# Layer 2 keys and values turned by VectorE in blocks and through DRAM, states in column groups of TensorE, and a planner in which VectorE and GpSimd exclude each other

## The chip, the cores and the metric

The kernel runs on one core of a Trainium2 chip. A core has five engines with queues of their own: TensorE (PE; its weight loads are shown as PEld), VectorE (DVE), ScalarE (ACT), GpSimd (POOL) and SyncE (SP), which here only issues DMAs. TensorE multiplies a stationary block (the weights, here up to 128 rows by 128 columns) with moving columns and writes to PSUM, which the kernel uses as eight banks of 128 x 512 float32. The metric is the device time of one execution in microseconds (us), as a median of several runs. A time of the profile is counted from the start of the span, the stretch that the profiler records.

## The reference

Two layers work on 1024 prompt tokens and on 8 sequences of 4 sample tokens with a state of their own, together 1056 tokens (TOK) of 1024 features. What is computed, cut to what matters:

```
xn = rmsnorm(x);  u = xn @ a_w_in                          # first layer: RG-LRU
xb, gate = u[:, :1536], u[:, 1536:]
xc = causal convolution of xb, 4 taps
r, i = sigmoid(block-diagonal products of xc + bias)
a = exp(-8 * softplus(-lam) * r)
h[t] = a[t] * h[t-1] + sqrt(1 - a[t]**2) * i[t] * xc[t]
x = x + (h * silu(gate)) @ a_w_out

xn = rmsnorm(x);  q, f, v, gate = split(xn @ b_w_in, 4)    # second layer: HGRN2, 8 heads of 128
g = lb + (1 - lb) * sigmoid(f);  k = 1 - g;  q = silu(q)   # a gate for each of the 128 key features
S[t] = diag(g[t]) @ S[t-1] + outer(k[t], v[t])             # a 128 x 128 state per head
o[t] = q[t] @ S[t]
x = x + (rmsnorm(o) * silu(gate)) @ b_w_out
y = rmsnorm(x)
```

The outputs are y and the final states of both layers, for the prompt and for the samples.

## The kernel before, in words

**Layout.** Activations lie with the features on the 128 partitions and the tokens along the free dimension. A product is made as three matmuls of rounded parts (`mm3`, lines L243 to L245: high by high, high by low, low by high), and each operand is split into a high and a low part on the other engines (`subtract`, L325). The first layer works in three chunks of 352 tokens, in the second most products go in quarters of 264 tokens.

**The planner.** The program of each layer isn't issued in the order of the source. Every operation is put into a `Flow` with its engine, an estimated time, the keys that it reads and writes and a priority. `Flow.plan` is a list scheduler: it takes again and again the engine that is free first and of its ready operations the one with the smallest key. `Flow.back` plans from the end backward, the resulting times become the keys of the next forward plan, and the best of nine forward plans sets the order in which every engine's instructions are emitted. `HOP` is the delay that the planner puts between engines, `side` an extra for TensorE work that isn't of the main chain. Main products (`main=True`) keep the order of the source. An operation marked `both` is one of VectorE that the planner stretches if GpSimd is busy. `search` changes keys at random, and keeps what lets an early operation of TensorE end no later; before the change only the first layer's flow uses it. A plan is only an order: on the chip every instruction waits for what it really depends on.

**Start.** 48 matmuls of ones (L729) stand ahead of the first products of layer 1; their result is not used.

**Layer 2.** The first two heads use plain products of 352 columns. For heads 2 to 7 `seven` forms two of the four projections at once, in seven products of half size in place of eight: the sums of the activations are built once (`add`, L1368, and a split), the sums of the weights for each head (`combine`, L1438). The sums of the seven products are made by VectorE as it reads them from PSUM (`plus`, L1501), over a ring of three banks. Each head has four bursts of other TensorE work between these products:

- burst 1: the parts of the attention matrix between neighbouring tokens (`levels01`: L1052 with L1072), and for the head before `keys_` and `values`;
- burst 2: the same over distances of 2 and 4 (`levels24`: L1052, L1086), `states` for the head before (L1217, and for the samples L1225), and `advance` (L1246);
- burst 3: `outs` for the head before (L1271, L1273), `advance`, and `levels816` (L1052, L1106);
- burst 4: `gated` for the head before, `levels3264`, and half of `values`.

Within a head the gates of tokens are multiplied up in a tree (`scale`: query and key rows in L1034, the gates themselves in L1043), level by level, and each burst needs the levels made after the burst before. `own_gate` (L1064) is the first step: queries times gates. `scale(h, 64, ...)` after burst 4 leaves in row B2 the keys, scaled to the end of their chunk of 128 tokens.

**Turning.** `states` computes for each chunk of 128 tokens the product of its keys and values, summed over tokens, so both are needed with tokens on the partitions. `transposed` has TensorE turn 128 x 128 blocks against an identity matrix into a PSUM bank (L1161, four to a bank), and ScalarE copies the bank to SBUF (L1167). That is done for all keys in burst 1 (8 blocks) and for the values in burst 4 (4 blocks) and burst 1 (4 blocks). `samples` does the same for the sample tokens (L1173). `states` then runs eight matmuls of 128 x 128 (L1217), and VectorE adds chunk after chunk with its decay (into `SA`). `kt` shares its buffer with `on`, the normed outputs that burst 4 turns back.

**DMA.** Nearly all transfers go through SP's queue, in the order of the plan (the helper `dma`, L312): the weights of `seven` into the slots `wraw` and a part of `R`, the states of the samples in (`si`) and out (`out_ss`), the gated outputs to a scratch in DRAM (`yd`).

The functions concerned, with their line numbers:

## Time and profile before

| | |
|---|---|
| three runs | 1072.68, 1069.47, 1072.20 us, median 1072.2 |
| profiled execution | 1069.42 us, its span 1067.3 us |
| granted clock of TensorE, mean | 0.996 |
| TensorE busy | 1054.5 us, 99% of the span |
| TensorE weight loads | 1026.1 us, 96% |
| VectorE busy | 816.2 us, 76% |
| ScalarE busy | 589.2 us, 55% |
| GpSimd busy | 526.4 us, 49% |
| instructions of TensorE | 9964 matmuls, as many weight loads |
| moved by DMA | 103.06 MB, mean 97 GB/s |

How to read it: busy time counts instructions that run, not those that wait. The page divides the span into 40 slices of 26.7 us and gives the busy share of each engine in each slice as a digit. The chain of waits follows the work that ended last back to the start, from each instruction to what released it. The timeline lists groups of neighbouring instructions of a kind: start and duration in us, engine, line, operation, the tiles written and read, and in square brackets how long the engine stood idle ahead of it and what ended that. In the tables by windows each engine has its busy microseconds, with the number of instructions in brackets, then the granted clock, the share of the DMA engines and the GB/s.

### The profile page before, as it was taken

The page shows a single profiled execution, that of the slowest core. Times are in us where ns is not written, and L with a number is a line of the kernel's source. Part 1 is how long each engine was busy: PE and PEld are TensorE (multiplying, and loading weights), DVE is VectorE, ACT ScalarE, POOL GpSimd, SP SyncE. Part 2 cuts the span into 40 slices and gives each one's busy share as a digit, 9 for nine tenths or more (in the row PEclk, how much of TensorE's full clock was granted, in tenths as well). Part 3 has the DMA queues.
Part 4 walks back from the last instruction along what each step waited for, and adds up shares of the span by engine and source line. Part 5 has one row for each costly group of instructions (what it writes and reads, how often), then busy time and mean ns, then how long its engine had stood idle before and what let it go on. Part 6 is the DMA issues. An engine that isn't in the chain of part 4 may idle for free.

```text
span 1067.3 us, 25614 instructions
## 1 busy us (share of the span) xinstructions
PE 1054.5 (99%) x9964; PEld 1026.1 (96%) x9964; DVE 816.2 (76%) x1610; ACT 589.2 (55%) x1340; POOL 526.4 (49%) x601
## 2 busy tenths in 40 slices
PE   9999999999999999999989999999999999999997
PEld 9999999999999999999989999999999999999986
DVE  7999995788888689264798987877868686883436
ACT  6569656877675875243344464646464554652324
POOL 3426443444634365555657555555545455552544
PEclk9999999999999999999999999999999999999998
DMA  9201112123752585440211121212121212374204
GB/s 294 67 20 52 57 47 74 56 60 97 228 173 61 171 282 179 126 131 28 80 33 40 44 91 46 90 44 91 44 92 51 74 62 65 123 214 127 78 8 163
DMA packets 70120, 103.06 MB, mean 97 GB/s; under 512 B 9200, under 2 KB 50160, under 8 KB 70000
## 3 DMA queue, kind: packets, MB, share of 16 engines
q1 hardware_dynamic: 67696, 98.67, 29.6%
q10 hardware_dynamic: 2304, 2.77, 0.7%
q8 instruction: 78, 1.28, 0.5%
q14 instruction: 42, 0.34, 0.1%
HBM read 71.05 MB, written 25.49 MB: 90 GB/s over the span
## 4 chain that ended last, share of the span: by engine, by line
PE 90%; DVE 6%; issue 1%; DMA 1%; POOL 1%; ACT 0%; ACTq 0%; POOLq 0%; DVEq 0%
PE mm L243 25%; PE mm L244 24%; PE mm L245 24%; PE hg L1052 1%; PE hg L569 1%; PE hg L1271 1%; DVE R L1368 1%; PE hg L1217 1%; PE hg L1161 1%; PE hg L243 1%; PE hg L245 1%; PE hg L244 1%; PE hg L1273 1%; DMA wraw<-in_w_dram 1%; PE mm L1052 1%
## 5 line engine op out<-in xcount | busy, mean ns | idle before, releaser
L243 PE MATMUL mm<-xh,whi 128*128 128x352 f32 (+1 forms) x1143 | 359.5, 315 | 0.0
L244 PE MATMUL mm<-xl,whi 128*128 128x352 f32 (+1 forms) x1143 | 354.8, 310 | 0.0
L245 PE MATMUL mm<-xh,wlo 128*128 128x352 f32 (+1 forms) x1143 | 354.7, 310 | 0.0
L325 POOL TENSOR_TENSOR wlo<-wraw,whi 128x256 fp32r<-128x256 f32 (+3 forms) x184 | 199.2, 1100 | 189.7 <-ACT whi L380 104.5
L244 PEld LDWEIGHTS mm<-xl,whi 128*128 128x128 f32 x1143 | 215.8, 189 | 1.7
L243 PEld LDWEIGHTS mm<-xh,whi 128*128 128x128 f32 x1143 | 215.5, 189 | 1.8
L245 PEld LDWEIGHTS mm<-xh,wlo 128*128 128x128 f32 x1143 | 215.5, 189 | 0.0
L501 DVE SCALAR_TENSOR_TENSOR k<-xb,prm_sb,k 128x352 f32<-128x352 f32 (+2 forms) x144 | 89.2, 629 | 14.8 <-ACT k L498 10.8
L243 PE MATMUL mm<-t,whi 128*128 128x264 f32 (+1 forms) x306 | 89.4, 292 | 0.5 <-DVE k L1501 0.5
L244 PE MATMUL mm<-t,whi 128*128 128x264 f32 (+1 forms) x306 | 87.7, 287 | 0.0
L245 PE MATMUL mm<-t,wlo 128*128 128x264 f32 (+1 forms) x306 | 87.6, 286 | 0.0
L1501 DVE TENSOR_TENSOR k<-mm,k 128x264 f32<-128x264 f32 x144 | 60.4, 428 | 34.5 <-PE mm L245 32.7
L584 POOL TENSOR_TENSOR k<-X 128x352 f32<-128x352 f32 x36 | 44.4, 1243 | 45.1 <-DVE R L585 34.3
L325 POOL TENSOR_TENSOR wlo<-R,whi 128x256 fp32r<-128x256 f32 x64 | 51.8, 830 | 25.4 <-ACT whi L1428 25.4
L380 ACT CAST whi<-wraw 128x512 fp32r<-128x512 f32 (+2 forms) x83 | 45.9, 574 | 26.4 <-PE mm L244 18.7
L243 PEld LDWEIGHTS mm<-t,whi 128*128 128x128 f32 x306 | 57.6, 188 | 1.2 <-DVE k L1501 0.9
L245 PEld LDWEIGHTS mm<-t,wlo 128*128 128x128 f32 x306 | 57.6, 188 | 0.0
L244 PEld LDWEIGHTS mm<-t,whi 128*128 128x128 f32 x306 | 57.6, 188 | 0.0
L243 PE MATMUL mm<-yh,whi 128*128 128x352 f32 x153 | 49.9, 326 | 0.0
L1428 ACT CAST whi<-wraw 128x512 fp32r<-128x512 f32 x52 | 32.0, 616 | 31.7 <-PE mm L245 17.4
L244 PE MATMUL mm<-yl,whi 128*128 128x352 f32 x153 | 49.4, 323 | 0.0
L245 PE MATMUL mm<-yh,wlo 128*128 128x352 f32 x153 | 49.4, 323 | 0.0
(478 smaller groups left out, 2601.3 us busy)
## 6 DMA issues: line engine op xcount, KB each, us to landing
wraw<-in_w_dram SPq DMA_DIRECT2D x90, 256.0 KB, 2.7
wraw<-in_wo_dram SPq DMA_DIRECT2D x34, 192.0 KB, 2.5
si<-in_s_in_dram SPq DMA_DIRECT2D x8, 512.0 KB, 3.6
out_ss_out_dram<-si SPq DMA_DIRECT2D x8, 512.0 KB, 2.8
R<-in_w_dram SPq DMA_DIRECT2D x15, 256.0 KB, 2.5
sg<-x1b SPq DMA_DIRECT2D x21, 176.0 KB, 2.8
x<-sg SPq DMA_DIRECT2D x21, 176.0 KB, 1.8
R<-td SPq DMA_DIRECT2D x72, 44.0 KB, 1.9
```

The source lines that it names most:

```text
L243: T.matmul(out, wh, xh, start=first, stop=False)
L244: T.matmul(out, wh, xl, start=False, stop=False)
L245: T.matmul(out, wl, xh, start=False, stop=last)
L325: emit = lambda: e.tensor_tensor(b, x, a.bitcast(F32), op=ALU.subtract)
L380: act(m, lambda hi=hi, raw=raw, m=m: S.copy(hi[:, :m], raw[:, :m]), rk, (hk,), prio)
L501: dve(u, lambda src=src, dst=dst, sh=sh, k=k: V.scalar_tensor_tensor(dst, sh(src, k), pc("cw", 12 * k + m), dst, op0=ALU.mult, op1=ALU.add ...
L569: fl.add("PE", 0.62, lambda ps=ps, i=i, c=c: T.matmul(ps[:96, :CH], gs[:, i, :], ST[:96, chunk(c)], start=True, stop=True), (("gs",), *((" ...
L584: pool(CH, lambda x=x, a=a, b=b: G.tensor_tensor(x, a.bitcast(F32), b.bitcast(F32), op=ALU.add), (ak, bk), (xk,), 3)
L1052: T.matmul(ps[32 * j:32 * j + 32, n * w:n * w + w], B[:, o:o + 32], q(slice(o, o + 32)), start=True, stop=True, tile_position=(0, 32 * j))
L1161: T.transpose(ps[:, n * 128:(n + 1) * 128], row[:, a:a + 128], ident)
L1428: act(512, lambda: S.copy(hi, raw), (rk,), (hk,), 2)
L1501: dve(QT, lambda: V.tensor_tensor(o[0], z[0], u[0], op=ALU.add), (z[1], u[1]), (o[1],), 0)
```

## The change

It has two parts.

**The planner.** `HOP` becomes a number for each engine. A Flow can be given `busy`, the times at which the engines are free as it begins; layer 2's is made from the log of layer 1's. In `plan` an operation of VectorE marked `both` starts to run only when the last operation of GpSimd is through (less 0.085 us), and an operation of GpSimd only when the last marked one of VectorE is through (less 0.05 us). The estimated times of many operations are other numbers. An empty operation of GpSimd writes the keys of the gate row ahead of layer 2, and layer 2's flow is searched too. The order of the main products, what the operations compute and how many there are is the same for layer 1.

**Layer 2.** `transposed` is gone. `turned` has VectorE turn a row of 1024 tokens by 32 x 32 blocks (one instruction of 128 x 1024, L1166 in the new file), writes the 512 KB to a scratch in DRAM, of which there are two for keys and two for values, and reads them back with four DMAs of 128 KB, one for each group of 32 partitions, so that whole columns of tokens lie on the partitions. It is called behind burst 4 for values and keys. In `kt` and `vt` the 128 features of a chunk are then four runs of 32. `states` takes the keys as four weight blocks of 32 columns, each in a column group of its own (`tile_position=(0, 32 * a)`), so there are 32 matmuls of 128 x 32 weights a bank in place of 4 of 128 x 128 (32 in place of 8 a head; the trace counts two instructions for each of these float32 matmuls). The values are read as four runs of 32 columns, in `states` and in `outs`.

```diff
-    HOP = 0.2
+    HOP = {"PE": 0.22, "DVE": 0.14, "ACT": 0.14, "POOL": 0.14, "SP": 0.2}
...
-    def __init__(self, until=None, side=1.2):
+    def __init__(self, until=None, side=1.2, busy=None):
...
+        self.busy = {e: (busy or {}).get(e, 0.0) for e in self.ENGINES}
...
-        return self.HOP + b[6] + (2.15 + a[5] / 250.0 if a[5] else 0.0)
+        return self.HOP[a[0]] + b[6] + (2.15 + a[5] / 250.0 if a[5] else 0.0)
...
-        free = dict.fromkeys(self.ENGINES, 0.0)
-        dma = 0.0
+        free = dict(self.busy)
+        dma = locked = taken = 0.0
...
-            if both and free["POOL"] > t0:
-                us = max(us, free["POOL"] - t0 + us - 0.13)
+            if both:
+                us += max(0.0, taken - t0 - 0.085)
+                locked = t0 + us
+            elif e == "POOL":
+                us += max(0.0, locked - t0 - 0.05)
+                taken = t0 + us
...
-            fl.add("ACT", 0.25 + 0.0007 * n + more, emit, r, w, prio)
+            fl.add("ACT", 0.08 + 0.00086 * n + more, emit, r, w, prio)
...
-            fl.add("DVE", 0.13 + 0.0011 * n, emit, r, w, prio, both=both)
+            own = 0.13 if "scalar_tensor_tensor" in emit.__code__.co_names else 0.075
+            fl.add("DVE", own + 0.00104 * n, emit, r, w, prio, both=both)
...
-            fl.add("POOL", 0.1 + 0.00245 * n, emit, r, w, prio)
+            fl.add("POOL", 0.13 + 0.0022 * n, emit, r, w, prio)
...
-        fl = Flow(side=0.4)
+        last = {e: max(t[3] for t in fl.log if t[1] == e) for e in Flow.ENGINES}
+        fl = Flow(side=0.4, busy={e: max(0.0, t - last["PE"]) for e, t in last.items()})
...
+        fl.add("POOL", 0.0, lambda: None, (), GK, 0)
...
-        def transposed(row, rk, dst, key, parts):
-
-            got = []
-            for i in parts:
-                ps, pk = next(hg)
-
-                def emit(i=i, ps=ps):
-                    for n in range(4):
-                        a = (4 * i + n) * 128
-                        T.transpose(ps[:, n * 128:(n + 1) * 128], row[:, a:a + 128], ident)
-
-                pe(0.49, emit, rk, (pk,))
-                got.append((i, ps, pk))
-            yield
-            for i, ps, pk in got:
-                act(512, lambda i=i, ps=ps: S.copy(dst[:, 4 * i:4 * i + 4, :].rearrange("p n d -> p (n d)"), ps), (pk,), ((key, i),), 2)
+        def turned(h, row, rk, dst, key, keys):
+
+            d = turn[key, h % 2]
+            dve(1024, lambda: V.transpose(dst, row[:, :1024].rearrange("p (n b i) -> p b n i", n=8, b=4)), rk, keys, 3, True)
+            dma(d, dst, keys, ((key, "d", h % 2),), 3, 512)
+            back = d.rearrange("(a i) (b m) -> b i a m", a=4, b=4)
+            for b in range(4):
+                dma(dst[32 * b:32 * b + 32].rearrange("p (a m) -> p a m", a=4), back[b], ((key, "d", h % 2),), (keys[b],), 3, 128)
...
                 def emit(i=i, ps=ps):
                     for n in range(4):
-                        T.matmul(ps[:, n * 128:(n + 1) * 128], kt[:, 4 * i + n, :], vt[:, 4 * i + n, :], start=True, stop=True)
-
-                pe(0.94, emit, (("kt", i), ("vt", i)), (pk,))
+                        for a in range(4):
+                            w = slice(32 * a, 32 * a + 32)
+                            T.matmul(ps[w, n * 128:(n + 1) * 128], kt[:, 4 * i + n, a], vt[:, 4 * i + n], start=True, stop=True,
+                                     tile_position=(0, 32 * a))
+
+                pe(1.05, emit, (*KK, *VK), (pk,))
...
-                        T.matmul(o, at[:, m, :], vt[:, m, :], start=True, stop=m == 0)
+                        T.matmul(o, at[:, m, :], vt[:, m], start=True, stop=m == 0)
...
-            run(together([*([gated(h - 1, *s)] if h else []), *([levels3264(h, *s), values(h, (0,))] if h < H else [])]))
+            run(together([*([gated(h - 1, *s)] if h else []), *([levels3264(h, *s)] if h < H else [])]))
+            if h < H:
+                turned(h, VT, [("VT", c) for c in range(4)], vflat, "vt", VK)
+                turned(h, *brow(h, 0), kflat, "kt", KK)
...
-            fl.run()
+            fl.run(SEARCH, 60.0)
```

The new file numbers its lines some 3 to 11 higher or lower: L1052 becomes L1063, L1034 becomes L1045, L1064 becomes L1075, L1217 becomes L1216, L1368 becomes L1371, L1501 becomes L1504, L243 becomes L248, L312 becomes L317.

In the listings that follow a row is an instruction or a row of like ones with their count: line, operation, tile written and tiles read, shape.

TensorE, the work of burst 1 in a steady head, before (`hg` and `mm` are PSUM banks, `sg` a row that holds keys or values, `krep` and `vrep` the sample tokens):

```order
L1052 MATMUL hg<-R,a 32x64 x32
L1072 MATMUL hg<-R,a 32x64
L1161 MATMUL hg<-ident,sg 128x128 x8
L1173 MATMUL hg<-ident,krep 96x128
L1161 MATMUL mm<-ident,sg 128x128 x4
L1173 MATMUL hg<-ident,vrep 96x128
L243 MATMUL mm<-t_5205,whi 128x264
```

and with the change:

```order
L1063 MATMUL hg<-R,a 32x64 x32
L1083 MATMUL hg<-R,a 32x64
L1176 MATMUL hg<-ident,krep 96x128
L1176 MATMUL hg<-ident,vrep 96x128
L248 MATMUL mm<-t_5205,whi 128x264
```

The twelve turns of keys and values are gone, and the next product follows the sample tokens. TensorE in burst 2 of such a head, before:

```order
L1052 MATMUL hg<-R,a 32x32 x32
L1086 MATMUL hg<-R,a 32x32
L1052 MATMUL hg<-R,sg 32x32 x32
L1217 MATMUL hg<-sg,kt 128x128 x8
L1225 MATMUL hg<-si,ab 32x128 x8
L1246 MATMUL mm<-vb,kst 128x512
```

and with the change:

```order
L1063 MATMUL hg<-R,a 32x32 x32
L1097 MATMUL mm<-R,a 32x32
L1063 MATMUL hg<-R,sg 32x32 x32
L1216 MATMUL hg<-sg,kt 32x128 x32
L1225 MATMUL mm<-si,ab 32x128 x8
L1246 MATMUL hg<-vb,kst 128x512
```

The eight products of keys and values have become 32 with a quarter of the weight columns. VectorE at the start of layer 2, before (`xh`, `xl` are the parts of the normed activations, `tmp` and `R` take the sums of `build`):

```order
L460 SCALAR_TENSOR_TENSOR sg<-sg,prm_sb,hg 128x352
L325 TENSOR_TENSOR xl<-sg,xh 128x352 x3
L1064 TENSOR_TENSOR R<-R,ST 128x1056
L961 MEMSET ssq 128x9
L1043 TENSOR_TENSOR sg<-ST 128x528
```

and with the change:

```order
L331 TENSOR_TENSOR xl<-sg,xh 128x352
L466 SCALAR_TENSOR_TENSOR sg<-sg,prm_sb,hg 128x352
L1371 TENSOR_TENSOR R<-xh 128x264 x2
L1371 TENSOR_TENSOR tmp<-tmp,xl 128x264
L1371 TENSOR_TENSOR R<-R,xl 128x264
L1371 TENSOR_TENSOR tmp<-xh 128x264
L1371 TENSOR_TENSOR tmp<-tmp,xl 128x264 x2
L1371 TENSOR_TENSOR R<-R,xl 128x264
L1075 TENSOR_TENSOR R<-R,ST 128x1056
L1054 TENSOR_TENSOR sg<-ST 128x528
```

Sums of `build` have moved ahead of the product of queries and gates. VectorE behind burst 4 of a steady head, with the change (the last scaling of the keys is the row L1045):

```order
L1045 TENSOR_TENSOR sg<-sg 128x8x64
L1504 TENSOR_TENSOR k<-mm,k 128x264
L1253 SCALAR_TENSOR_TENSOR si<-si,gp,hg 128x128 x4
L1504 TENSOR_TENSOR k<-mm,k 128x264
L1166 STREAM_TRANSPOSE kt<-sg 128x1024
L1504 TENSOR_TENSOR k<-mm,k 128x264
L1325 SCALAR_TENSOR_TENSOR sg<-mm,prm_sb,sg 128x512
L1441 TENSOR_TENSOR wraw<-wraw 128x512
```

The turn of the keys stands two evictions and four updates of the sample states behind their last scaling. SP's queue in a steady head, before:

```order
L312 DMA out_ss_out_dram<-si 128x1024
L312 DMA si<-in_s_in_dram 128x1024
L312 DMA yd<-sg 128x1056
L312 DMA wraw<-in_w_dram 128x512 x2
L312 DMA R<-in_w_dram 128x512
L312 DMA wraw<-in_w_dram 128x512 x2
L312 DMA out_sp_out_dram<-a 128x128
```

and with the change, where the first two rows write and read the values and the rows with `kt` the keys:

```order
L317 DMA vt<-sg 128x1024
L317 DMA sg<-vt 32x4x256 x4
L317 DMA out_ss_out_dram<-si 128x1024
L317 DMA kt<-kt 128x1024
L317 DMA yd<-sg 128x1056
L317 DMA wraw<-in_w_dram 128x512
L317 DMA si<-in_s_in_dram 128x1024
L317 DMA wraw<-in_w_dram 128x512
L317 DMA kt<-kt 32x4x256 x4
L317 DMA R<-in_w_dram 128x512
L317 DMA wraw<-in_w_dram 128x512 x2
L317 DMA out_sp_out_dram<-a 128x128
```

Ten DMAs have come in between the old ones; those behind the key write wait in the queue until it is issued, those behind the four reads until the write has landed.

More of the change, by code (lines that the diff above doesn't have):

```diff
@@ L400, in emit @@
                         mm3(ps[:, :CH], w(k)[:2], *xs[k][:2], k == 0, k == n - 1)
-                fl.add("PE", 0.48 * len(ks), emit, (*(q for k in ks for q in (*xs[k][2], *w(k)[2])), *more), (pk,), 1, main=True)
+                fl.add("PE", 0.484 * len(ks), emit, (*(q for k in ks for q in (*xs[k][2], *w(k)[2])), *more), (pk,), 1, main=True)
             return ps, pk
@@ L736, in seq @@
             for eng, emit in emits:
-                fl.add(eng, 0.2, emit, (("P",),), keys, prio, both=eng == "DVE")
+                fl.add(eng, 0.1, emit, (("P",),), keys, prio)
         def smalls():
@@ L955, in tile_trunk @@
         Bs, Gs, B2, VT, Gc = a_rows[0], ST, rows[2], rows[0], rows[4]
-        vt = rows[5][:, :1024].rearrange("p (n d) -> p n d", n=8)
+        vflat = rows[5][:, :1024]
+        vt, kt = (o.rearrange("p (a n j) -> p n a j", a=4, n=8) for o in (vflat, kflat))
+        VK, KK = ([(o, i) for i in range(4)] for o in ("vt", "kt"))
+        turn = {(o, i): nc.dram_tensor(f"{o}_{i}", (128, 1024), F32, kind="Internal").ap() for o in ("vt", "kt") for i in range(2)}
         SA = a_rows[1]
@@ L959, in tile_trunk @@
                            (ab, 288, [("ab",)])):
-            pool(0.3 * n, lambda o=o: G.memset(o, 0.0), (), keys, 3)
+            pool(0.7 * n, lambda o=o: G.memset(o, 0.0), (), keys, 3)
         dve(9, lambda: V.memset(ssq, 1.0), (), [("ssq", i) for i in range(3)], 3)
@@ L1179, in samples, with values @@
                 act(128, lambda: S.copy(whole, ps[:32]), (sk,), (("vts",),), 2)
-        def values(h, parts, s=None, sk=None):
-            vk = [("VT", c) for c in range(4)]
-            gens = [transposed(VT, vk, vt, "vt", parts)]
-            if s is not None:
-                gens.append(samples(vrep, "vrep", s, sk, 192, vst, "vst", 2, vts))
-            yield from together(gens)
-            if s is not None:
-                masked(0)
+        def values(h, s, sk):
+            yield from samples(vrep, "vrep", s, sk, 192, vst, "vst", 2, vts)
+            masked(0)
         def masked(i):
@@ L1198, in keys_ @@
         def keys_(h, s, sk):
-            B, bk = brow(h, 0)
-            yield from together([transposed(B, bk, kt, "kt", (0, 1)), samples(krep, "krep", s, sk, 64, kst, "kst", 1)])
+            yield from samples(krep, "krep", s, sk, 64, kst, "kst", 1)
         def together(gens):
@@ L1245, in advance @@
             ps, pk = next(hg)
-            pe(0.25, lambda: T.matmul(ps, kst, vb.rearrange("p b v -> p (b v)"), start=True, stop=True),
+            pe(0.36, lambda: T.matmul(ps, kst, vb.rearrange("p b v -> p (b v)"), start=True, stop=True),
                (("kst",), ("vb",)), (pk,))
@@ L1331, in burst1 @@
             s = next(hg)
-            run(together([*([levels01(h, *s)] if h < H else []), *([keys_(h - 1, *s), values(h - 1, (1,), *s)] if h else [])]))
+            run(together([*([levels01(h, *s)] if h < H else []), *([keys_(h - 1, *s), values(h - 1, *s)] if h else [])]))
         def burst2(h):
@@ L1648, in tile_trunk @@
         spare = []
-        for o, olds in ((R[:, 0], eight("A", 1)), (SA, [("SA", i) for i in range(2)]), (rows[5], [("vt", i) for i in range(2)]),
+        for o, olds in ((R[:, 0], eight("A", 1)), (SA, [("SA", i) for i in range(2)]), (rows[5], VK),
                         (SG[6], ykeys(0, 0, TOK))):
```

52 lines of the change are left out of this document (26 added, 26 removed).

## The prediction, made before the changed kernel was run

> **What bounds the kernel now.** I read the busy shares and the slices first, then the chain of waits, then the windows of two steady heads, and last the timeline of the bursts that the change touches.
>
> ```profile
> PE 1054.5 (99%) x9964; PEld 1026.1 (96%) x9964; DVE 816.2 (76%) x1610; ACT 589.2 (55%) x1340; POOL 526.4 (49%) x601
> DVE  7999995788888689264798987877868686883436
> PEclk9999999999999999999999999999999999999998
> PE 90%; DVE 6%; issue 1%; DMA 1%; POOL 1%; ACT 0%; ACTq 0%; POOLq 0%; DVEq 0%
> ...
> core 0: us, PE busy (x) PEld busy (x) DVE busy (x) ACT busy (x) POOL busy (x), PEclk, DMA share, GB/s
> 733.50:790.20 56.70, 56.70 (x807) 54.81 (x807) 43.90 (x97) 30.17 (x79) 29.80 (x38) 1.00 0.21 68
> 790.20:846.90 56.70, 56.70 (x807) 54.81 (x806) 43.90 (x97) 30.16 (x79) 29.78 (x38) 1.00 0.20 68
> ```
>
> TensorE is busy 99% and carries 90% of the chain. A steady head of layer 2 takes 56.70 us, the same in both rows, and TensorE fills all of it, while VectorE is free for 56.70 - 43.90 = 12.8 us. So time that leaves TensorE in layer 2 leaves the kernel, unless another engine then makes it wait.
>
> TensorE really waits in the middle of the run at one place, the start of layer 2 (the timeline, then windows):
>
> ```profile
> 514.31 1.27 DVE L1064 TENSOR_TENSOR R<-R,ST 128x1056 f32<-128x1056 f32 x1 [7.58 <-POOL ST L721]
> 539.34 2.85 DVE L1368 TENSOR_TENSOR R<-R,xl 128x264 f32<-128x264 f32 x2
> 538.93 2.97 POOL L325 TENSOR_TENSOR wlo<-wraw,whi 128x512 fp32r<-128x512 f32 x2 [0.26 <-PE hg L1052]
> 545.79 0.76 PE L1052 MATMUL hg<-R,sg 128*32 128x32 f32 x64 [2.88 <-DVE sg L1034]
> 547.09 0.73 PE L1106 MATMUL hg<-R,a 128*16 128x16 f32 x64 [0.53 <-DVE a L1034]
> ...
> 546.00:548.00 2.00, 1.47 (x129) 1.35 (x116) 1.97 (x5) 0.75 (x2) 0.00 (x0) 0.64 0.03 8
> 548.00:550.00 2.00, 2.00 (x8) 2.00 (x9) 2.00 (x5) 1.23 (x2) 0.00 (x0) 0.51 0.00 0
> ```
>
> VectorE sits idle for 7.58 us before L1064, since GpSimd's gate row is late. Then it is behind: two sums of L1368 take 2.85 us beside GpSimd's work, though 264 columns cost it some 0.45 us alone (the L1501 rows below, of the same width). TensorE waits 2.88 + 0.53 = 3.41 us for L1034, and after it the granted clock is 0.64 and 0.51 over 4 us, which loses 0.36 x 2 + 0.49 x 2 = 1.7 us more. That place costs 5.1 us.
>
> **The change, part by part.** The sum is made against the profiled execution, 1069.4 us (span 1067.3 and 2.1 around it). The three runs shown are 1069.47, 1072.20 and 1072.68, so the middle of all four executions is 1070.8, which is 1.4 above the profiled one.
>
> *Transposes leave TensorE.* One steady head (burst 4, burst 1, burst 2):
>
> ```profile
> 793.55 0.66 PE L1161 MATMUL mm<-ident,sg 128*128 128x128 f32 x4
> 793.96 0.37 PE L243 MATMUL mm<-t,whi 128*128 128x264 f32 x1
> ...
> 808.77 1.10 PE L1052 MATMUL hg<-R,a 128*32 128x64 f32 x64
> 809.69 0.28 PE L1072 MATMUL hg<-R,a 128*32 128x64 f32 x2
> 809.90 1.09 PE L1161 MATMUL hg<-ident,sg 128*128 128x128 f32 x8
> 810.83 0.38 PE L1173 MATMUL hg<-ident,krep 128*96 128x128 f32 x2
> 811.04 0.60 PE L1161 MATMUL mm<-ident,sg 128*128 128x128 f32 x4
> 811.48 0.38 PE L1173 MATMUL hg<-ident,vrep 128*96 128x128 f32 x2
> ...
> 821.85 2.05 PE L1217 MATMUL hg<-sg,kt 128*128 128x128 f32 x16
> 823.83 0.65 PE L1225 MATMUL hg<-si,ab 128*32 128x128 f32 x16
> 824.40 0.50 PE L1246 MATMUL mm<-vb,kst 96*128 96x512 f32 x1
> ```
>
> Matmuls overlap, so I take start to next start: 0.41 (793.55 to 793.96), 0.93 (809.90 to 810.83) and 0.44 us (811.04 to 811.48), together 1.78 us a head. Eight heads: -14.2 us, nothing beside it, as TensorE has no gap there.
>
> *States in column groups.* L1217 now takes 16 instructions and 1.98 us (821.85 to 823.83), 124 ns each. After the change there are 64 instructions a head, of 32 weight columns by 128 moving columns. L1225, next row, has that form already: 16 in 0.57 us, 36 ns each, which makes 64 x 36 = 2.28 us. That 0.57 includes the change back to the full array. L1052 at 808.77 has 64 of them, half as wide, in 0.92 us, 14.4 ns each, or 28.8 for the double width: 1.84 us. The ends per head are -0.14 and +0.30 us; I take 2.06 us, the middle, so +0.08 x 8 = +0.6 us (ends -1.1 and +2.4). The values are now read by L1217 and L1271 as four runs of 32 columns; L1052's 64 wide reads are two such runs already, so no extra is taken.
>
> *VectorE turns both, 16 instructions of 128x1024.* No row shows this operation. From below: L1064 does 1056 columns in 1.27 us alone (514.31 above), 1.23 for 1024. From above, the same line beside GpSimd:
>
> ```profile
> 787.22 0.43 DVE L1501 TENSOR_TENSOR k<-mm,k 128x264 f32<-128x264 f32 x1 [0.42 <-PE mm L245]
> 797.43 0.69 DVE L1034 TENSOR_TENSOR sg<-sg 128x512 f32<-128x512 f32 x1
> 799.42 0.68 DVE L1438 TENSOR_TENSOR R<-R,wraw 128x512 f32<-128x512 f32 x1
> 801.66 1.79 DVE L1064 TENSOR_TENSOR R<-R,ST 128x1056 f32<-128x1056 f32 x1
> 815.56 1.21 DVE L1438 TENSOR_TENSOR R<-wraw,R 128x512 f32<-128x512 f32 x1
> ...
> 800.25 0.33 SPq L312 DMA_DIRECT2D wraw<-in_w_dram  x1
> 809.24 0.33 SPq L312 DMA_DIRECT2D wraw<-in_w_dram  x1
> ...
> out_ss_out_dram<-si SPq DMA_DIRECT2D x8, 512.0 KB, 2.8
> wraw<-in_wo_dram SPq DMA_DIRECT2D x7, 128.0 KB, 2.2
> ...
> L1167 ACT COPY kt<-hg x12: 587/592/602, 576.0 to 975.9; 128x512 f32<-128x512 f32 x12
> ```
>
> I take 1.25, near the lower end, because it reads one tile and not two: 2.5 us a head, against 12.8 us free. So VectorE goes to 46.4 of some 55.0 us and the cost is nothing; if that cover went, behind the transposes stand the evictions L1501, three banks deep, and TensorE behind those. [...]
>
> *ScalarE* loses four copies of 0.59 us a head (L1167). It had 26 us free, so nothing is gained.
>
> *The way via DRAM, ten DMAs a head on SP's queue.* Each issue is 0.33 us, so 3.3 us in 55. Keys are the late ones. The last scaling of the key row (L1034, 797.43) ends at 798.1; in the new order two evictions (0.86) and four state updates (1.1) stand between it and the turn (1.25), so it ends near 801.3. The write, 512 KB, takes 0.33 + 2.8; the four reads, 128 KB each, 4 x 0.33 + 2.2: they land near 808.0. L1217 begins at 821.85 - 1.78 = 820.1. That leaves 12 us. SP then also holds back weight loads behind the wait for the write. Before, those loads go at 800.25 (when L1438 frees the slot) to 809.24, and their first reader, L1438, runs at 815.56. With the key reads ahead of two of them they go at about 807 to 811, and land 2.7 us later: about 2 us are left. Cost nothing, with little to spare. The load rises by 2 MB a head on a share of 0.2.
>
> *The planner.* It now makes VectorE and GpSimd wait for each other, and knows when each engine is free as layer 2 begins. In the new order ten L1368 sums stand ahead of L1064, some 4.5 us in the 7.58 us that were idle, and no sum stands between the four scalings that burst 3 waits for. So the 3.41 us of waiting and the slow clock should go. What is late next is burst 3's second half: scaling, copy and hand-over after burst 2 come to about the 3.9 us of product between them. I leave 1.1 us there: -4.0 us (ends 0 and -5.1).
>
> *The first 45 us.* The 48 filler matmuls L729 stay, 46 in one block before and now in pieces between the first products:
>
> ```profile
> 1.03 13.49 PE L729 MATMUL hg<-ones 128*128 128x128 f32 x92 [1.03 <-DVE nr L442]
> 14.28 0.41 PE L243 MATMUL mm<-xh,whi 128*128 128x352 f32 x1
> 32.65 0.43 PE L243 MATMUL mm<-xh,yh 128*128 128x352 f32 x1 [0.40 <-DVE sg L529]
> 42.30 0.43 PE L244 MATMUL mm<-xl,X 128*128 128x352 f32 x1 [0.33 <-DVE xl L325]
> ```
>
> TensorE's work is the same, so only new waits count. The old ones are 0.40 and 0.33 us. A product that starts four microseconds earlier can find its operands not there. I take 0, ends -0.7 and +4. The rest of layer 1 has no gap to win; a wait can only be added there. I take 0, ends 0 and +6 (a gap like that of layer 2's start, 5.1, and a little).
>
> Sum: 1069.4 - 14.2 + 0.6 - 4.0 = 1051.8 for an execution like the profiled one, and 1.4 more for the middle of several: 1053 us.
>
> **The rivals.**
> *New waits in layer 1 or at the start.* VectorE is near 9 in each of the slices from 27 to 160 us, and the new order puts some 3 us of other VectorE work ahead of the first L529, which is the eviction that TensorE waited for at 32.65. Against it: only the waits listed stand in those slices before. [...]
> *The time stays within 0.3%* (which is what a measurement of this kernel can tell from no change). The layer 2 gain would have to be given back as 1.8 us of waiting per head, from weight loads held behind the key write on SP: 2 us of room are left, so a write 4 us late does it. About 1070.
> *Slower, by the key hand-over.* If the keys land after 820.1, L1217 waits in each head. The delay that decides is 12 us, plus 2.2 us a head for the (14.2 + 4.0 - 0.6) given back: from 14 us on it is slower, and each further microsecond costs 8. At 15 us about 1077 us. For it: ten DMAs in a queue that waits in order. Against it: DMAs of this size land in 2 to 3 us.
> *Slower, because weight loads of column groups are not hidden.* An L1225 load takes 110 ns:
>
> ```profile
> L1225 PEld LDWEIGHTS hg<-si,ab x112: 106/110/110, 591.8 to 988.4; 128*32 128x32 f32 x112
> ```
>
> If each of 64 loads stood alone, the states would take 7.0 us, +5.0 a head, +40 in all: 1092 us. L1225's own pace of 36 ns with that load speaks against it. It decides above 64 ns per instruction. [...]
>
> **How the numbers follow.** Forecast, 1047 to 1059: 0.68. New waits, 1059 to 1069: 0.17. Within 0.3%: 0.05. Late keys: 0.07. Weight loads: 0.03. Faster is 0.68 + 0.17 = 0.85, same 0.05, slower 0.10. The lower end is 1069.4 - 14.2 - 1.1 - 5.1 - 0.7 = 1048.3, and 1047 for a little more; the upper end, 1067, leaves out the two slower cases, the unchanged one and the worst of the new waits.
>
> **What would show it.** A steady head at about 55.0 us with TensorE full and VectorE near 46.4. L1216 with 64 instructions in some 2.1 us. Keys landed some 10 us before L1216 begins, and SP with no weight load that ScalarE waits for. At the start of layer 2 no wait of over a microsecond, and a clock of 1.00 behind it. The start within a microsecond of before. The prediction is wrong if the steady head stays over 56, if TensorE shows waits for VectorE between 27 and 530 us, or if the turn on VectorE takes over 5 us.

## The result: no change that can be measured

The changed kernel takes 1070.58 us (median of 12 runs, 1068.52 to 1075.0) against 1072.03 us before (12 runs). The ratio of the means is 0.9997, with a 95% interval from 0.9983 to 1.0011. Forecast were 1053 us, with 1047 to 1067 as the range. The profiled execution has a span of 1069.7 us, against 1067.3 before.

The order of the main products is the same in both kernels, so the same matmul can be looked up in both traces. The table gives the start of the n-th of their 5976 matmuls (three to a product, so that matmul 96 begins the 33rd product, which the expectations below call the 32nd) before, and how much later it starts after the change and in the first four experiments, in us. Each column is one profiled execution; executions of one kernel lie up to 4 us apart (1068.68 to 1072.68 before), so a difference of a microsecond or two between two columns at the end of the table is not read.

| matmul | place | before | after | e1 | e2 | e3 | e4 |
|---|---|---|---|---|---|---|---|
| 0 | first product | 14.28 | -3.56 | -3.79 | -0.45 | -1.39 | 0.05 |
| 96 | 33rd product | 32.65 | 8.03 | 7.95 | 0.02 | 0.73 | 0.13 |
| 180 | 61st product | 48.04 | 12.00 | 11.96 | 0.03 | 0.72 | 1.68 |
| 600 | layer 1 | 119.65 | 13.29 | 14.92 | 0.02 | 0.72 | 1.77 |
| 3060 | end of layer 1 | 531.55 | 13.29 | 15.16 | 0.02 | 0.72 | 2.61 |
| 3240 | behind the start of layer 2 | 569.78 | 8.99 | 10.94 | 0.66 | -2.84 | -2.19 |
| 4392 | middle of layer 2 | 770.93 | 9.40 | 12.68 | -2.77 | -4.92 | -5.27 |
| 5640 | end of layer 2's heads | 993.82 | 2.57 | 14.11 | -9.46 | -11.46 | -11.72 |
| 5975 | last | 1056.50 | 2.41 | 13.95 | -9.46 | -11.46 | -11.86 |

So layer 2 did bring a gain, 13.3 - 2.4 = 10.9 us, though less than the forecast 17.6; and the first 75 us, for which the sum had 0, took 13 us.

The page of the changed kernel, parts 1, 2 and 4:

```profile
PE 1045.4 (98%) x10220; PEld 1013.1 (95%) x10220; DVE 817.2 (76%) x1626; ACT 574.2 (54%) x1308; POOL 520.1 (49%) x601
PE   9899999999999999999999999999999999999997
DVE  8999667589698788454697899787878787995436
PE 85%; DVE 9%; issue 2%; DMA 1%; POOL 1%; ACT 0%; SPq 0%; ACTq 0%; POOLq 0%; DVEq 0%
```

TensorE is busy 9 us less, yet the span is longer, so it waits more. VectorE's part of the chain has grown from 6% to 9%. TensorE's waits (the view of waits by line: in all, times, longest) and its timeline in the first 41 us say where:

```profile
PE hg L284 <- DVE R L441: 2.7, 2, 1.9
PE hg L1216 <- DMA kt<-kt: 2.4, 1, 2.4
PE hg L461 <- DVE k L459: 1.9, 2, 1.4
PE hg L1216 <- issue: 1.8, 2, 1.1
PE hg L284 <- DVE xb L441: 1.2, 1, 1.2
```

```profile
23.27 0.78 PE L284 MATMUL hg<-ones,xb 128*128 128x1 f32 x6 [1.20 <-DVE xb L441]
30.34 0.78 PE L284 MATMUL hg<-ones,R 128*128 128x1 f32 x6 [1.88 <-DVE R L441]
34.11 0.86 PE L461 MATMUL hg<-k,ones 128*128 128x352 f32 x2 [1.43 <-DVE k L459]
37.67 0.78 PE L284 MATMUL hg<-ones,R 128*128 128x1 f32 x6 [0.82 <-DVE R L441]
39.26 0.86 PE L461 MATMUL hg<-k,ones 128*128 128x352 f32 x2 [0.48 <-DVE k L459]
40.68 0.66 PE L248 MATMUL mm<-xh,yh 128*128 128x352 f32 x1 [0.56 <-DVE sg L535]
```

L284 sums the squares of a chunk for its normalization and L461 spreads the result; VectorE prepares both (L441, L459) and comes late, as it does with L535, which takes a product out of its PSUM bank: six waits in 18 us. After these waits, and again after three of 0.4 to 0.6 us from 54.5 to 57.5 us, the granted clock falls (from 1.00 at 34 to 38 us to 0.77 at 42 to 46, and from 1.00 at 50 to 54 us to 0.63 at 58 to 62). The windows of these stretches, and of one steady head of layer 2 (its first and second group of seven products, then both):

```profile
38.00:42.00 4.00, 2.96 (x13) 2.20 (x13) 3.95 (x12) 1.58 (x4) 2.07 (x3) 0.81 0.56 180
42.00:46.00 4.00, 4.00 (x21) 4.00 (x21) 4.00 (x10) 2.64 (x5) 2.23 (x3) 0.77 0.20 66
58.00:62.00 4.00, 4.00 (x18) 4.00 (x18) 4.00 (x9) 3.63 (x9) 1.09 (x2) 0.63 0.04 11
```

```profile
780.34:808.85 28.51, 28.51 (x390) 27.40 (x389) 21.02 (x48) 17.55 (x51) 15.12 (x17) 1.00 0.26 91
808.85:835.45 26.60, 26.54 (x451) 25.68 (x450) 23.70 (x52) 10.14 (x25) 14.45 (x20) 1.00 0.40 127
780.34:835.45 55.11, 55.05 (x839) 53.09 (x838) 44.72 (x99) 27.69 (x75) 29.58 (x37) 1.00 0.33 108
```

The clock of 0.81, 0.77 and 0.63 over three times 4 us loses at most 0.19 x 4 + 0.23 x 4 + 0.37 x 4 = 3.2 of the 13.3 us (in the first of the windows TensorE also stood idle). An undisturbed head takes 55.11 us, where some 55.0 were forecast, but not all heads are undisturbed.

### The profile page after: what moved, and what is told of

Its sections match the earlier page's. It is cut to its first block, busy times and chain, and to the rows that moved or that the text cites. A ratio compares the mean times of both kernels' runs of the same rounds, so it can differ in the third digit from the quotient of the medians.

```text
span 1069.7 us, 26257 instructions
## 1 busy us (share of the span) xinstructions
PE 1045.4 (98%) x10220; PEld 1013.1 (95%) x10220; DVE 817.2 (76%) x1626; ACT 574.2 (54%) x1308; POOL 520.1 (49%) x601
## 3 DMA queue, kind: packets, MB, share of 16 engines
q10 hardware_dynamic: 2304, 2.77, 0.7%
## 4 chain that ended last, share of the span: by engine, by line
PE 85%; DVE 9%; issue 2%; DMA 1%; POOL 1%; ACT 0%; SPq 0%; ACTq 0%; POOLq 0%; DVEq 0%
PE mm L248 24%; PE mm L250 23%; PE mm L249 23%; PE hg L1216 2%; PE hg L1063 1%; PE hg L1271 1%; PE hg L575 1%; DVE sg L466 1%; PE hg L1273 1%; DVE xl L331 1%; PE hg L249 1%; PE hg L250 1%; PE hg L248 1%; DVE k L507 1%; DVE R L441 1%
## 5 line engine op out<-in xcount | busy, mean ns | idle before, releaser
L248 PE MATMUL mm<-xh,whi 128*128 128x352 f32 (+1 forms) x1143 | 358.6, 314 | 0.0
L248 PEld LDWEIGHTS mm<-xh,whi 128*128 128x128 f32 x1143 | 215.5, 189 | 1.7
L507 DVE SCALAR_TENSOR_TENSOR k<-xb,prm_sb,k 128x352 f32<-128x352 f32 (+2 forms) x144 | 87.0, 615 | 23.0 <-ACT k L504 19.9
L248 PE MATMUL mm<-t,whi 128*128 128x264 f32 (+1 forms) x306 | 89.6, 293 | 0.1
L1504 DVE TENSOR_TENSOR k<-mm,k 128x264 f32<-128x264 f32 x144 | 60.1, 424 | 23.4 <-PE mm L250 21.7
L331 POOL TENSOR_TENSOR wlo<-R,whi 128x256 fp32r<-128x256 f32 x64 | 56.0, 895 | 28.1 <-ACT whi L1431 27.1
L248 PEld LDWEIGHTS mm<-t,whi 128*128 128x128 f32 x306 | 57.5, 188 | 0.9 <-ACT krep L1003 0.3
L248 PE MATMUL mm<-yh,whi 128*128 128x352 f32 x153 | 51.3, 336 | 0.0
```

The source lines that it names most:

```text
L248: T.matmul(out, wh, xh, start=first, stop=False)
L331: emit = lambda: e.tensor_tensor(b, x, a.bitcast(F32), op=ALU.subtract)
L507: dve(u, lambda src=src, dst=dst, sh=sh, k=k: V.scalar_tensor_tensor(dst, sh(src, k), pc("cw", 12 * k + m), dst, op0=ALU.mult, op1=ALU.add ...
L1504: dve(QT, lambda: V.tensor_tensor(o[0], z[0], u[0], op=ALU.add), (z[1], u[1]), (o[1],), 0)
```

## The experiments

**e1 to e4: which part of the change took the 13 us, and which brought the gain.** e1 has the planner's part alone, e2 the layer 2 code alone (in the diff below, e1 is all but these lines, e2 these lines with all that belongs to them):

```diff
-        def transposed(row, rk, dst, key, parts):
+        def turned(h, row, rk, dst, key, keys):
...
-                        T.matmul(ps[:, n * 128:(n + 1) * 128], kt[:, 4 * i + n, :], vt[:, 4 * i + n, :], start=True, stop=True)
+                        for a in range(4):
...
+                turned(h, VT, [("VT", c) for c in range(4)], vflat, "vt", VK)
+                turned(h, *brow(h, 0), kflat, "kt", KK)
```

> The planner's part alone: its rules, costs, free times and search are the new ones for both layers, while keys and values are still turned by TensorE and the states are still products of 128 x 128. Theory A (the new order of the first 75 us costs 13.3 us, the new order at the start of layer 2 gains 4.4 us, and neither has to do with the turning): the first products fall 13 us behind by 80 us, the wait of 2.9 us at the start of layer 2 is gone, a steady head is still 56.7 us, so about 9 us slower than before, some 1081 us. Rival B (the loss at the start comes with the new layer 2 code, not with the planner): no loss at the start, 1067 to 1068 us.

> The layer 2 code alone: keys and values turned by VectorE and through DRAM, states in column groups, with the old planner for both layers. Theory A: the start as before, the wait at the start of layer 2 as before, and the heads shorter by what TensorE no longer does, 1.8 us each less what new waits take: 1058 to 1065 us. Rival B: a loss of about 13 us in the first 80 us, no faster than 1070 us. If the hand-over through DRAM were the loss, L1216 would wait some microseconds in each head and the time would stay at 1070 or above with an undisturbed start.

e1 took 1083.18 us, 1.0095 times before (1.0072 to 1.0119), 2 us above what theory A said. e2 took 1059.25 us, 0.9873 (0.9855 to 0.9891), as A said. The table above shows e1 with the loss at the start and e2 without it, so rival B falls. e2 has the gain in the heads and none at the start of layer 2 (0.02 and 0.66 at matmuls 3060 and 3240); e1 has the gain at that start (15.16 and 10.94) and none in the heads. e1 also loses 3 us between the start and the end of layer 2's heads: the new plan is a little worse there for the old code.

e3 and e4 set back layer 1's planning in the changed kernel, e3 all of it, e4 the estimated times alone (the formulas below, those written beside single operations, and with them the mark `both` of layer 1's small operations on parameters):

```diff
-        return self.HOP[a[0]] + b[6] + (2.15 + a[5] / 250.0 if a[5] else 0.0)
+        return (0.2 if Flow.first else self.HOP[a[0]]) + b[6] + (2.15 + a[5] / 250.0 if a[5] else 0.0)
...
+            if Flow.first:
+                if both and free["POOL"] > t0:
+                    us = max(us, free["POOL"] - t0 + us - 0.13)
+            elif both:
...
-            fl.add("DVE", own + 0.00104 * n, emit, r, w, prio, both=both)
+            fl.add("DVE", 0.13 + 0.0011 * n if Flow.first else own + 0.00104 * n, emit, r, w, prio, both=both)
```

> The changed kernel, with layer 1 alone planned by the old rule, costs and delays; layer 2 as changed. Theory A: the products run as before up to 530 us, and all that layer 2 gains shows: 1070.6 - 13.3 = 1057 us. Rival C (an earlier layer 1 is waited for elsewhere, so that layer 2 gives the time back): 1065 us or above.

> The changed kernel, with only the estimated times of layer 1's operations set back; the exclusion of VectorE and GpSimd and the new delays between engines stay. Theory A1 (the numbers of the operations spoil the start): the start is no more than 3 us behind before, 1057 to 1061 us. Theory A2 (the exclusion or the delays spoil it): 10 us or more behind by 80 us, 1068 to 1072 us.

e3 took 1056.82 us, 0.9851 (0.9833 to 0.987); e4 1057.99 us, 0.9865 (0.9845 to 0.9884). Both come out as theories A and A1 said. With the old estimated times the start is 1.7 us behind before at the 61st product, though VectorE and GpSimd exclude each other in that plan too. So the loss at the start comes with the new estimated times and that mark (in a plan that has the exclusion; no run has the new times without it), and an undisturbed start lets all that layer 2 gains come through. e3 is the fastest of these, 1.5% faster than before.

**e5, e6, e9: what the new estimates do to the start.** Up to the start of the 61st product VectorE was busy 41.53 us before and 54.48 us after (windows of before, then after):

```profile
0.00:48.04 48.04, 46.29 (x299) 45.33 (x299) 41.53 (x93) 30.05 (x63) 18.88 (x26) 1.00 0.63 200
```

```profile
0.00:60.04 60.04, 51.05 (x300) 47.71 (x301) 54.48 (x145) 33.79 (x72) 20.05 (x33) 0.95 0.51 161
```

TensorE does about the same matmuls in both (299 and 300); it stands idle 9.0 us in place of 1.75 and is busy 4.8 us longer, at a mean clock of 0.95. VectorE does 52 instructions more, 13 us of work. That alone proves little, since a VectorE that is nearly full does more in any longer stretch. The 33rd product is a better place: in both kernels TensorE waits there until VectorE has come to the instruction that takes an older product out of its bank (L529, L535). Up to there (before, then after):

```profile
0.00:32.65 32.65, 31.22 (x206) 30.72 (x207) 26.46 (x61) 21.18 (x46) 11.73 (x18) 1.00 0.76 246
```

```profile
0.00:40.68 40.68, 33.27 (x214) 31.25 (x215) 35.19 (x102) 22.87 (x49) 13.28 (x21) 1.00 0.71 226
```

So 41 more instructions of VectorE, 8.7 us of work, stand ahead of a product that is 8.0 us late. Among the first to stand ahead are small operations on parameters (most 12 columns wide), which the new numbers count at 0.1 us (0.2 before, and exclusive with GpSimd). Up to the 33rd product there are 34 of these on one line, 9.0 us in all, against 10 and 2.3 us before; on the chip most take some 0.17 us and a few up to 1.2 us (the two largest groups of that line after the change, up to 40.68 us; busy time and mean in ns stand behind the bar):

```profile
L747 DVE TENSOR_SCALAR smalls<-smalls 128x12 f32<-128x12 f32 x12 | 4.3, 358 | 0.2
L747 DVE TENSOR_TENSOR smalls<-smalls 128x12 f32<-128x12 f32 x10 | 2.7, 274 | 0.3
```

I took these for the cause (theory S). e5 changes one number of the plan, and e6 one formula, in layer 1 only:

```diff
-                fl.add("PE", 0.484 * len(ks), emit, ...
+                fl.add("PE", (0.48 if Flow.first else 0.484) * len(ks), emit, ...
```

```diff
-            fl.add("DVE", own + 0.00104 * n, emit, r, w, prio, both=both)
+            fl.add("DVE", 0.13 + 0.0011 * n if Flow.first else own + 0.00104 * n, emit, r, w, prio, both=both)
```

> The changed kernel, with one number of layer 1's plan set back: a product of layer 1 counts 0.48 us again, not 0.484. The plan is another one by that: it puts the 100th product 4 us earlier than the changed kernel's plan does, where the plan of before has it, but still 46 of VectorE's small parameter operations ahead of the 32nd product (13 before). Theory S (these small operations, which the plan counts at 0.1 us and the chip runs in 0.27, delay the first normalization): 7 us or more behind before at 75 us, 1067 to 1072 us. Rival P (the plan as a whole was a bad one, and its own forecast tells): at most 2 us behind, 1057 to 1060 us.

> The changed kernel, with the formula for VectorE's operations set back in layer 1 (0.13 + 0.0011 n); the small operations still count 0.1 us. The plan puts 20 of them ahead of the 32nd product, where before had 13 and the changed kernel 46. Theory S: 2 to 5 us behind before at 75 us, 1058 to 1062 us. Were it the exclusion or the delays between engines: 10 us behind, 1067 us or more.

e5 took 1068.44 us, 0.9974 (0.9965 to 0.9984), and is 9.3 us behind at the 33rd product and 9.7 at the 61st; the forecast of its own plan, which had it level with before, did not come true on the chip. e6 took 1062.72 us, 0.9925 (0.9903 to 0.9947), and is 3.8 and 4.9 us behind. Both are as S said at the 75 us (9.6 and 5.1 us behind, e6 at the edge), e6 a little above its time. So VectorE's formula alone gives back 7.1 of the 12.0 us at the 61st product. e9 keeps all new numbers, and holds the small operations back:

```diff
-        smalls()
         begin(0, 0, 2)
         begin(1, 2, 6)
         products(0)
+        held = fl.main
+        smalls()
...
                 fl.add(eng, 0.1, emit, (("P",),), keys, prio)
+                fl.ops[-1][3].add(held)
```

> The changed kernel with all its new numbers, but the small parameter operations (and those that build the masks) may be planned only behind the 48th product: they are added later and carry a dependency in the plan, no wait on the chip. Theory S: the 32nd product, 8.0 us behind before in the changed kernel, is within 1.5 us of before. The plan itself then puts the 60th product 4 us later than before's, by the convolution's operations, so some 5 us are lost later: 1060 to 1066 us. Were the small operations not the cause: 32nd product 5 us behind or more, 1068 us or more.

e9 took 1072.56 us, 0.9999 (0.9988 to 1.001). It misses on both counts: the 33rd product is 3.6 us behind and not 1.5, the 61st 14.3 us. Held back, they give 4.4 of the 8.0 us at the 33rd product back (8.03 against 3.60), but the plan then puts something else ahead. Up to the 61st product VectorE is busy 50.4 us, 8.9 more than before, and idle 11.9, 5.4 more, so its amount of work isn't the whole of it, and other waits stand in their place:

```profile
PE mm L248 <- ACT xh L467: 3.6, 1, 3.6
PE mm L248 <- DVE sg L535: 3.2, 1, 3.2
PE hg L284 <- DVE R L441: 2.4, 1, 2.4
```

So theory S was too narrow. What the runs show is that in this kernel the order made with the new numbers is the worse one at the start, and that several numbers of them matter (a change of the product's estimate by 0.8% moved the 61st product by 2.3 us). Why the new numbers lead there I didn't settle.

**e7, e8, e10 and its mended form (e12): the waits inside the states.** In e3, TensorE's waits in burst 2 have no releaser ("issue"), but for one of 0.4 us for the keys. There are four: 1.25 and 0.66 us in the products of keys and values, 0.63 and 0.67 us in those of the samples, 3.2 us together (the expectation of e10 has 2.8). The timeline of the third of the eight states in e3:

```profile
702.90 0.92 PE L1223 MATMUL hg<-sg,kt 128*32 128x128 f32 x25
705.08 1.19 PE L1223 MATMUL hg<-sg,kt 128*32 128x128 f32 x36 [1.25 <-issue]
```

I counted TensorE's instructions in the order of the trace, weight loads, matmuls and semaphore instructions. In the changed kernel, e2, e3 and e4, such waits stand at instructions 8386, 11714 and 16833 or one beside them, at different times, and in some of them also at 9921 and 13505: counted off in blocks of 256, all at 193 or 194 of a block. In e1, with the old code of layer 2, no wait stands there. In e3, a packet of 16 KB of the instruction queue q8 starts at 702.68 us, 2.4 us before the matmul goes on at 705.08; in the sixth head it is 2.4 us as well. The page has 80 such packets, and the 20571 recorded instructions of TensorE are 80.4 times 256 (before the change 78 packets and 78.3 times, in e7 81 and 80.8), so I take each packet for the fetch of one such block of TensorE's program:

```profile
q8 instruction: 80, 1.31, 0.5%
```

Theory I is that TensorE has run through its program faster than the next block came. e7 and e8 shift the stream by repeating one small matmul, e10 pulls the dense part apart:

```diff
-            pe(0.1, lambda: T.matmul(s[:32, :32], B1[:, 1024:], A1[:, 1024:], start=True, stop=True), (*a1k, *b1k), (sk,))
+            pe(0.1, lambda: [T.matmul(s[:32, :32], B1[:, 1024:], A1[:, 1024:], start=True, stop=True) for _ in range(1 if h else 33)], (*a1k, *b1k), (sk,))
```

```diff
-GV = "126b74b35", "12b675b43", "126b754b3"
+GV = "126b74b35", "12b675b43", "126b75b4b3"
...
+        def burst2a(h):
+            s = next(hg)
+            run(together([levels24(h, *s)]))
+
+        def burst2b(h):
+            s = next(hg)
+            run(together([states(h - 1, *s), advance(h - 1, 0)]))
```

> e3 (layer 1 planned as before) with 128 more instructions in TensorE's stream: a small matmul of burst 2 of the first head is made 33 times, with the same result, and the orders of all engines stay. In e3 all waits of TensorE in the states that have no releaser stand at one place of the stream, instruction 193 or 194 of a block of 256. Theory I (TensorE waits for the next block of 256 instructions): the waits in the third and the sixth of the eight states (705 and 873 us in e3, 1.3 and 0.7 us) go, others come where the blocks now end, in the second and the seventh (near 648 and 928 us); 1055 to 1060 us, 1 to 2 of that for the matmuls themselves. Rival K (the keys' way through DRAM or the column groups make the waits): the same heads wait, 1058 us.

> As the run before it, with 192 more instructions. Theory I: the blocks end inside the states only in the second head (at their start) and the fifth, so waits there at most, and none in the third and the sixth; 1055 to 1059 us. Rival K: waits in the third and the sixth, as in e3.

> e3 (layer 1 planned as before) with burst 2 of heads 3 to 8 in two: the levels where they were, states and advance two products later. The instructions are the same, but between the two dense parts stand two products with 5.8 us for 96 instructions. Theory I (a block of 256 instructions takes 2.4 us or more to come, and the dense burst uses one up faster than that): the waits without a releaser in the states, 2.8 us in e3, are under 1 us, 1053 to 1056 us. Rival K (the column groups or the keys make them): they stay, 1056 to 1058 us.

> As e10, with the copy of the samples' queries (which e10 made one burst too early, so that its samples' outputs are those of other queries) behind the states again; nothing else is changed. Theory I: as e10, no wait without a releaser in the states of heads 3 to 7, 1053 to 1056 us. Rival K: such waits of 2 us or more, 1056 to 1058 us.

In e7 the waits of the third and sixth states are gone (one of 0.23 us is left ahead of the sixth), and those of the second and seventh have come, at 10178 and 18625, again 194 and 193 of a block. These are the second, the third and the seventh:

```profile
649.84 0.96 PE L1223 MATMUL hg<-sg,kt 128*32 128x128 f32 x26 [0.93 <-issue]
...
703.90 1.96 PE L1223 MATMUL hg<-sg,kt 128*32 128x128 f32 x64
...
929.25 0.71 PE L1223 MATMUL hg<-sg,kt 128*32 128x128 f32 x17 [1.82 <-issue]
```

Two more of 0.48 and 0.53 us, which I had not named, stand in the fourth and the fifth, at 193 and 194 too. e7 took 1061.13 us, 0.9911 (0.9887 to 0.9935), a little above its range. In e8 the heads were not those that I had named (waits of 0.58, 1.35 and 0.71 us in the third, fifth and seventh), since the traces had not shown me which blocks have a wait; but all three are at 193 or 194 of a block. It took 1058.23 us, 0.9879 (0.986 to 0.9898). The third head, where I expected none, had its wait at that place of a block seven matmuls ahead of the states' own end.

e10, whose outputs for the samples are those of other queries, took 1055.22 us, 0.9845 (0.9829 to 0.9862), and the mended form 1056.25 us, 0.9865 (0.9849 to 0.9882), a little above what theory I said and inside rival K's range. But in neither is there a wait without a releaser in the states behind the first (0.73 and 0.63 us there), as I said and K did not. In both the largest now stands in the other half of the first split burst, in the levels ahead of the second states, at 193 of a block again (1.58 us in e10, and this in the mended form):

```profile
646.03 0.25 PE L1070 MATMUL hg<-R,sg 128*32 128x32 f32 x3 [1.97 <-issue]
```

From matmul 3720 to 5640, behind that wait, the mended form gains 10.1 us on before and e3 7.5 us; the 2.6 us between them are as long as the three waits that e3 has there (1.25, 0.67 and 0.66 us). With the new wait ahead of that stretch, waits without a releaser are 2.6 us in all against 3.2 in e3: splitting the burst has moved them more than removed them, and the medians of e3 and of the mended form don't differ by more than their runs do. Rival K falls by the places, and not by the times: column groups and the way through DRAM are the same in all of these.

In all kept traces with the new code of layer 2 together, TensorE has 39 waits of over 0.25 us without a releaser. All are in burst 2, all at 193 or 194 of a block, and before each a fetch of 16 KB had begun 2.2 to 3.0 us earlier. That the fetch is what they wait for is inferred from this; whether the recording of the trace has a part in them was not tested. Most blocks have no such wait (in e3 four of some 80 have one), and the longest is 1.97 us, in the mended form.

## Why the prediction was wrong, by its own steps

**The first 45 us: the step that failed.** "TensorE's work is the same, so only new waits count ... I take 0, ends -0.7 and +4." The waits for VectorE and the slow clock behind them took 13.3 us in place of 0, 12.0 of them by the 61st product. I had seen that products start four microseconds earlier and that other VectorE work stands ahead of the first L529, counted it as some 3 us, and then took the near end. It was 8.7 us (35.19 against 26.46 up to the 33rd product), and VectorE, busy 41.5 of the first 48 us, had room for 6.5. e1 to e4 show that the planner's new estimated times for layer 1 make this order (e4 sets back the mark of the small operations with them); why they lead there stays open. The rival "New waits in layer 1 or at the start" had the place and the sign, but its ends of +4 and +6 are together less than 13.3, and it was given 0.17. No run shows the term for a slow clock that takes its range from there up to 1069; in the changed kernel the clock of 0.81, 0.77 and 0.63 stood behind waits of 0.4 to 1.9 us, and cost 3.2 us at most.

**Transposes leave TensorE, -14.2: right.** Burst 1 takes 1.56 us in place of 2.84, and the half of a head with burst 4 28.51 in place of 28.95: 1.72 a head against the 1.78 forecast.

**States in column groups, +0.6: the pace even better than its range, the sum wrong.** Undisturbed, the 64 instructions of a head (32 products, 16 to a bank and not the 32 that the description of the change has) take 1.74 us from their start to the next row's (27 ns each), below the lower end of 1.84:

```profile
940.91 1.95 PE L1216 MATMUL hg<-sg,kt 128*32 128x128 f32 x64
942.66 0.65 PE L1225 MATMUL mm<-si,ab 128*32 128x128 f32 x16
```

A weight load of L1216 takes 110 ns (median of 480), so 64 that stood alone would take 7.0 us, as the rival "Slower, because weight loads of column groups are not hidden" has it; with 27 ns from matmul to matmul they don't stand alone here. But burst 2 as a whole takes from 4.10 to 8.07 us after in the second to the seventh of the eight, against 4.18 before. The term was mis-sized: in place of +0.6, the burst costs some 7 us over the eight heads. Waits at 193 or 194 of a block are 2.3 us of that (0.45, 1.07 and 0.73 us), and the one late hand-over of keys, below, with the slow clock behind it 3.9.

**The hand-over of keys.** In a steady head the four reads are issued from 813.38 us, the last has landed at 818.51 and the states begin at 829.63, so the 12 us of room were about right (11.1). For the second of the eight states the reads are issued from 651.48 and take up to 8.7 us, among other transfers at 240 GB/s, and TensorE waits once (timeline, windows):

```profile
661.57 3.58 PE L1216 MATMUL hg<-sg,kt 128*32 128x128 f32 x64 [2.40 <-DMA kt<-kt]
```

```profile
650.00:660.00 10.00, 9.17 (x195) 8.92 (x194) 9.55 (x23) 3.21 (x8) 4.46 (x6) 1.00 0.87 240
660.00:664.00 4.00, 2.44 (x49) 2.47 (x53) 2.36 (x6) 1.69 (x3) 3.24 (x4) 0.71 0.01 4
```

That is 2.4 us and, with the clock at 0.71 behind it, states of 3.28 us in place of 1.74: what the rival "Slower, by the key hand-over" describes, in one head of eight. In e3 the same wait is 0.4 us.

**VectorE turns both: right.** The instruction takes 1.24 us, where I took 1.25 (my reason, that it reads one tile and not two, no run tests):

```profile
L1166 DVE STREAM_TRANSPOSE kt<-sg x8: 1233/1235/1245, 569.7 to 970.4; 128x1024 f32<-128x1024 f32 x8
```

**The start of layer 2, -4.0: right.** Between matmuls 3060 and 3240 the changed kernel gains 4.3 us. The longest wait left there is 0.74 us, and the clock behind it is 1.00.

**"Within 0.3%" came out, by another cause.** I had made it from 1.8 us of waiting in each head for weight loads on SP; it was the start that gave most of the gain back. That this rival's time came out is luck.

**Added up.** Start +13.3, start of layer 2 -4.3, transposes 8 x -1.72 = -13.8, burst 2 +6.9: together +2.1 us, against +2.4 in the table.

## What to carry to other kernels

Where an engine beside the bound one is nearly full, count how much of its work a new order puts ahead of the same product; "the same work" says nothing while the order decides who waits. A plan with better estimates need not be a better plan: e5 moved one estimate by 0.8% and its own forecast by 4 us, and the chip followed only in part (2.3 us at the 61st product), so look at the place where an engine can't catch up, and change that part of the plan by itself, as e3 does. Many small matmuls in a row are also a stream of instructions: where TensorE waits and nothing releases it, count whether the place repeats (here at 193 or 194 of every block of 256 that has a wait, for up to 1.97 us).

## What was unexpected of the hardware

TensorE, it seems, waits for its own program. All waits of over 0.25 us without a releaser lie at the same place of a block of 256 instructions, up to 2.0 us long, and other heads wait when the stream is shifted by 128 or 192 instructions (e7, e8); the matmul goes on 2.2 to 3.0 us after a fetch of 16 KB began. Before the change burst 2 had 163 matmuls in 4.18 us and no such wait, after it 211 in 4.10 us where undisturbed, with such waits in three of eight heads. What sets the moment at which the fetch begins is open, and so is why only some blocks are waited for.
